# Output projection of a hybrid decoder trunk: pieces of 512, 256 and 256 columns, and the last piece's residual added by products with an identity

## The chip, the core and the metric

The kernel runs on one core of one Trainium2 chip. A core has five engines with a queue of instructions each: TensorE (PE, the matrix products, with a weight-load stage PEld), VectorE (DVE), ScalarE (ACT), GpSimd (POOL) and SyncE (SP, which here only starts transfers). Each works through its own queue in program order and waits on semaphores for the others. Products write into PSUM, which has eight banks of 128 partitions x 512 float32; everything else lies in SBUF or in HBM. The metric is the device time of one execution in microseconds (us): 806.76 us before, the median of 3 runs.

## What is computed

Two decoder layers on 256 tokens of width 1024, in float32. Each normalises the stream, makes one wide projection, runs three token mixers, merges them under gates, and adds an output projection to the stream. Only the end of a layer matters here:

```python
for layer in range(DEPTH):                      # DEPTH = 2
    h = rms_norm(x, norm_w[layer])
    proj = jnp.einsum('bsd,de->bse', h, w_in[layer])
    ...
    branch = jnp.einsum('bsiw,iwd->bsid', ys, w_proj[layer])
    g = jax.nn.sigmoid(gates.reshape(b, s, N_BRANCH, d) + gate_bias[layer])
    merged = jnp.sum(g * branch, axis=2)
    x = x + jnp.einsum('bsd,de->bse', merged, w_out[layer])
return rms_norm(x, final_norm_w)
```

## The kernel before

**Products.** A float32 factor is carried as the sum of two parts in a 32-bit format that PE reads at its full rate (`fp32r`): a high part, copied by ACT, and a low part, the difference, made by DVE (`split`, L287). A product of two factors is three products: high x high, low x high, high x low, for each of the eight k (128 of the 1024 contracted rows). The 256 tokens are two tiles of 128, t = 0 and t = 1; a tile's transposed activations are the stationary side, the weights move.

**Weights** come in blocks of 128 x 1024 numbers (512 KB): `load_part` (L351) starts a transfer on SP's queue into one of six `raw` buffers, and `feed` (L383) splits a block into one of six `hi` and six `lo` buffers. A block of a 256-wide piece holds four k, one of a 512-wide piece two. `feed` runs when a block is released, and no further than `state["limit"]`.

**Order.** PE's order is written out by the code itself: `ops` is a list of steps in program order, and small jobs (`launch`, `pump`, `drain`, L115 to L180) are slipped in between by a clock that adds up the products' estimated lengths. A job's due time is its launch plus a delay, `D_H = (4.8, 6.4)` for the transposes of the next layer's input. DVE's, ACT's and POOL's orders come from the scheduler, in which `tc.high_priority()` and `pin` (L284, keep in program order) intervene.

**The end of a layer.** The last projection piece is merged with its gate, transposed and split (`u_proj`, `merge`, `mT`): the activations `y.mh`, `y.ml` of k = 4 to 7 of t = 1 are the last to be there. In `u_proj` (L1126) the limit is set to two blocks of the output weights before this last merge, then to a third. The output projection follows in three pieces of columns (L1380). The first one, `u_out2`, goes over both tiles in two halves of k: k 0 to 3 of t = 0, of t = 1, then 4 to 7 of each. Its first action is the transposes that are still due of t = 0; between the halves `late` runs the transposes of t = 1 and lifts the limit. The other two pieces are done tile by tile: both of t = 0, then both of t = 1 (L1383).

**Eviction** (`out_end`, L1202). DVE adds the residual `xo` to the bank into `y.xn`; ACT (for the very last piece DVE) sums the squares. After a tile's third piece follow the row's variance, a reciprocal root with a Newton step (`row_rsqrt2`), and, in layer 0, the next layer's input h by two scalings of 512 columns (L1236), whose transposes and splits (`hT`) are a job of the planner; they wait in `drain(5)` and `drain(6)` at the latest, ahead of layer 1's first products. In layer 1 the scaled rows go out by two transfers per tile: 640 columns scaled by DVE and sent by SP, 384 by ACT.

Of the kernel before, what the change touches and what calls it, by code (L numbers as in the profile page):

```python
# [16 lines left out]
P = 128  # L17
# [3 lines left out]
L = 2  # L21
# [29 lines left out]
def hybrid_trunk(  # L51
# [17 lines left out]
    def T(tag, shape, dtype=F32, bufs=None):  # L69
        count[0] += 1  # L70
        return sb.tile(shape, dtype, tag=tag, name=f"{tag}_{count[0]}",
                       bufs=bufs if bufs is not None else BUFS.get(tag, 1))
# [5 lines left out]
    def pmm():  # L78
        return PS("mm", 3)
# [169 lines left out]
    def row_rsqrt2(v, last):  # L249

        r0 = T("sm", [P, 8])
        if last:
            s = T("sm", [P, 8])
            act(s[:, 0:1], v, AF.Sqrt)
            nc.vector.reciprocal(r0[:, 0:1], s[:, 0:1])
        else:
            nc.gpsimd.tensor_tensor(r0[:, 0:1], v, mhalf[:, 0:1], op=ALU.pow)
        a = T("sm", [P, 8])
        stt(a[:, 0:1], r0[:, 0:1], v, r0[:, 0:1], op0=ALU.mult, op1=ALU.mult)
        r = T("rs", [P, 8], bufs=4)  # L260
        stt(r[:, 0:1], a[:, 0:1], -3.0, r0[:, 0:1], op0=ALU.add, op1=ALU.mult)
        return r
# [7 lines left out]
    def in_turn(ap):  # L270
        return ap.rearrange("p (a i) -> p i a", a=2)
# [8 lines left out]
    def halves(ap):  # L280

        return ap.rearrange("p (a i) -> p a i", a=2)

    def pin(f):  # L284
        return lambda *a, **k: tc.keep_in_program_order(f(*a, **k))  # L285
# [217 lines left out]
            if w.last and (k + 1) % w.kper == 0:  # L503
                release(w, k // w.kper + 1)

    def tok(ah, al, w, t, turn=True, mid=None):


        n = w.n
        p = pmm()  # L510
        b = in_turn if turn else lambda ap: ap
        if mid is None and n > 300:
            mid = pump
        dense(p[:, 0:n], lambda k: ah[:, t, k, :], lambda k: al[:, t, k, :], lambda k: b(w.hi(k)),
              lambda k: b(w.lo(k)), w, mid=mid)
        return ordered(p[:, 0:n]) if turn else p[:, 0:n]
# [661 lines left out]
    def u_out(y, c, t, i):  # L1178

        def f(w):  # L1180
            xo = out_start(y, c, t, i, w.n)
            out_end(y, c, t, i, w.n, xo, tok(y.mh, y.ml, w, t))
        return f

    def u_out2(y, c):

# [15 lines left out]
    def out_end(y, c, t, i, n, xo, p):  # L1202
        sl = slice(c, c + n)
        with tc.high_priority():
            tt(halves(y.xn[:, t, sl]), p, halves(xo), op=ALU.add)
            last = y.l + 1 == L
            if last and i == 2:
                junk = T("L2", [P, 512])
                nc.vector.tensor_tensor_reduce(out=junk[:, 0:n], in0=y.xn[:, t, sl], in1=y.xn[:, t, sl],
                                               scale=1.0, scalar=0.0, op0=ALU.mult, op1=ALU.add,  # L1210
                                               accum_out=y.ss[t][:, i:i + 1])
            else:
                sum_sq(y.xn, t, c, y.ss[t][:, i:i + 1], n)
            nwb = fin["w"] if last else layers[y.l + 1].nwb
            if i == 2:
                v = y.var[t][:, 1:2]
                pin(stt)(v, y.ss[t][:, 2:3], 1.0 / D, y.var[t][:, 0:1], op0=ALU.mult, op1=ALU.add)
            if last:
                pin(stt)(y.xn[:, t, sl], y.xn[:, t, sl], -0.5, nwb[:, sl], op0=ALU.mult, op1=ALU.mult)
            else:  # L1220
                nc.scalar.dma_start(xres[t * P:(t + 1) * P, sl], y.xn[:, t, sl])
            if i == 1:
                y.var[t] = row_var(y.ss[t], 2)
            if i == 2:
                r = row_rsqrt2(v, last)
                if last:
                    m = 640
                    ts(y.xn[:, t, 0:m], y.xn[:, t, 0:m], r[:, 0:1], None, op0=ALU.mult)
                    nc.sync.dma_start(out2[t * P:(t + 1) * P, 0:m], y.xn[:, t, 0:m])
                    act(y.xn[:, t, m:D], y.xn[:, t, m:D], AF.Copy, scale=r[:, 0:1])  # L1230
                    nc.scalar.dma_start(out2[t * P:(t + 1) * P, m:D], y.xn[:, t, m:D])
                else:
                    h = layers[y.l + 1].h[t] = T("L4", [P, D])
                    for j in range(2):
                        hs = slice(j * 512, (j + 1) * 512)
                        stt(h[:, hs], y.xn[:, t, hs], r[:, 0:1], nwb[:, hs], op0=ALU.mult, op1=ALU.mult)  # L1236
        if i == 2 and not last:
            launch(5 + t, hT(layers[y.l + 1], t), D_H[t])
        if i == 1:
            pump()  # L1240

    fin = {}

# [19 lines left out]
    def sub(src, n=256):  # L1263
        subs.append((src, n))
        return len(subs) - 1
# [5 lines left out]
    for y in layers:  # L1271
# [105 lines left out]
        op(None, load_final if l + 1 == L else lambda: layer_consts(layers[1], nc.gpsimd))  # L1377
        for f in fox:
            f()
        o = [sub([(0, w_out[l, :, c:c + n])], n) for c, n in ((0, 256), (256, 512), (768, 256))]  # L1380
        pieces_out[l] = o[0]
        op(o[0], u_out2(y, 0))
        for t in range(2):  # L1383
            for i, c in ((1, 256), (2, 768)):
                op(o[i], u_out(y, c, t, i))

    for i, (src, n) in enumerate(subs):
# [204 lines left out]
```

## Time and profile before

| | us |
|---|---|
| median of 3 runs | 806.76 |
| lowest, highest | 806.67, 806.95 |
| span of the profiled execution, first to last instruction | 805.1 |
| busy in it: PE, DVE, ACT, POOL | 796.5, 684.2, 533.8, 167.5 |
| layer 0's output projection on PE, from its first product to layer 1's first | 382.03 to 404.73 |
| layer 1's output projection on PE, first product to the end of the last | 776.84 to 798.84 |
| last instruction of DVE, end | 801.4 |

The profiled execution itself is known by its span; what lies around the span, 1.66 us against the median, is taken to stay as it is. A row of the timeline gives the start in us from the span's start, the busy time, the engine, the line of the kernel (often that of a helper), the operation, what is written and read, the shapes and the number of merged instructions; behind it, in brackets, how long the engine sat idle before and what released it. Instructions overlap at their ends, so from one row's start to the next is often less than the busy time.

### The profile page before, as it was taken

To read this page: it belongs to the slowest core of one execution; us is meant where nothing else is said; L and a number is where in the kernel's file an instruction comes from. 1 tells how busy PE (TensorE), PEld (TensorE's weight loads), DVE (VectorE), ACT (ScalarE), POOL (GpSimd) and SP (SyncE) were. 2 spreads that over 40 slices of the span, in tenths; PEclk is the share of its full clock that TensorE was granted. 3 is DMA by queue.
4 is the path that set the end of the run, shared out by engine and by line. 5 is a ranking of instruction groups with operands and counts; after the bars stand their busy time and mean duration, and the time that the engine had idled before them with its cause. 6 is when DMAs were issued, how large, how long until landed. Compare 5 with 4: busy or idle time off the path is not lost.

```text
span 805.1 us, 14840 instructions
## 1 busy us (share of the span) xinstructions
PE 796.5 (99%) x5160; PEld 711.6 (88%) x5160; DVE 684.2 (85%) x1416; ACT 533.8 (66%) x1146; POOL 167.5 (21%) x236
## 2 busy tenths in 40 slices
PE   9999999999999999999999999999999999999996
PEld 8998988888998988888998899888889989888896
DVE  6878999997998997795785799999889999969865
ACT  7776768875775885543665678687657768755452
POOL 3166213140210100033001741122311220002000
PEclk9999999999999999999999999999999999999999
DMA  9997987797765565686678987679976546576632
GB/s 316 280 259 172 253 219 200 219 290 220 198 184 167 174 187 170 219 253 205 217 251 257 239 210 217 157 217 287 285 211 196 183 143 202 156 248 210 209 106 78
DMA packets 138827, 170.43 MB, mean 212 GB/s; under 512 B 9353, under 2 KB 106465, under 8 KB 138753
## 3 DMA queue, kind: packets, MB, share of 16 engines
q1 hardware_dynamic: 114960, 140.53, 55.5%
q0 software_dynamic: 13328, 13.29, 10.3%
q10 hardware_dynamic: 10464, 15.67, 6.7%
q8 instruction: 41, 0.67, 0.3%
q14 instruction: 34, 0.27, 0.1%
HBM read 154.71 MB, written 2.16 MB: 195 GB/s over the span
## 4 chain that ended last, share of the span: by engine, by line
PE 91%; issue 3%; DMA 2%; POOL 2%; DVE 1%; ACT 1%; POOLq 0%; DVEq 0%
PE mm L109 78%; PE mx L109 9%; PE mx L113 4%; DMA L<-L 1%; DMA hb<-in_sinks_dram 1%; POOL L L488 1%; DMA L<-in_x_dram 0%; DVE L L551 0%; ACT pp L610 0%; POOL L L285 0%; POOL L L562 0%; DVE lo L291 0%; POOL sm L224 0%; POOL L L571 0%; POOL L L572 0%
## 5 line engine op out<-in xcount | busy, mean ns | idle before, releaser
L109 PE MATMUL mm<-L,hi 128*128 128x512 f32 x1056 | 354.7, 387 | 0.5 <-ACT L L487 0.3
L291 DVE TENSOR_TENSOR lo<-raw,hi 128x1024 fp32r<-128x1024 f32 (+1 forms) x276 | 313.3, 1154 | 40.9 <-ACT hi L290 36.1
L109 PE MATMUL mm<-hi,L 128*128 128x512 f32 (+2 forms) x1168 | 303.1, 349 | 0.1
L290 ACT ACTIVATE hi<-raw 128x1024 fp32r<-128x1024 f32 (+1 forms) x276 | 265.6, 982 | 50.6 <-PE mm L109 30.0
L109 PE MATMUL mm<-L,lo 128*128 128x256 f32 x1056 | 266.6, 273 | 0.0
L109 PEld LDWEIGHTS mm<-hi,L 128*128 128x128 f32 x1168 | 205.8, 190 | 23.2 <-issue 1.5
L109 PEld LDWEIGHTS mm<-L,hi 128*128 128x128 f32 x1056 | 195.1, 190 | 27.4 <-issue 3.0
L109 PEld LDWEIGHTS mm<-L,lo 128*128 128x128 f32 x1056 | 202.1, 191 | 5.3
L109 PE MATMUL mm<-lo,L 128*128 128x512 f32 (+2 forms) x584 | 201.5, 347 | 0.0
L109 PEld LDWEIGHTS mm<-lo,L 128*128 128x128 f32 x584 | 110.2, 190 | 10.7
L488 POOL DMA_DIRECT2D L<-L x68 | 60.7, 915 | 192.5 <-ACT L L487 155.2
L1074 POOL TENSOR_SCALAR_AFFINE_SELECT bias<-bias 128x128 f32<-128x128 f32 x64 | 30.8, 513 | 82.7 <-DMA bias<-cumd 82.7
L829 DVE SCALAR_TENSOR_TENSOR L<-L,vec,L 128x255 f32<-128x255 f32 (+2 forms) x96 | 46.2, 481 | 1.9 <-ACT L L826 0.4
L486 ACT ACTIVATE L<-mm 128x256 f32<-128x256 f32 x84 | 31.9, 380 | 20.0 <-PE mm L109 14.0
L652 ACT ACTIVATE pp<-pp,nm 128x128 f32<-128x128 f32 x64 | 28.2, 443 | 22.8 <-DVE nm L646 22.8
L1109 ACT ACTIVATE L<-L 128x512 f32<-128x512 f32 x24 | 15.1, 631 | 34.5 <-DVE L L1106 30.8
L610 ACT ACTIVATE pp<-pp,nm 128x128 f32<-128x128 f32 x32 | 12.6, 394 | 24.9 <-DVE nm L615 24.1
L488 POOL DMA_DIRECT2D qt<-L x16 | 14.2, 925 | 71.4 <-ACT qt L487 64.6
L1142 POOL TENSOR_TENSOR L<-L,L 128x512 f32<-128x512 f32 x8 | 12.0, 1494 | 74.0 <-DVE L L1141 74.0
L487 ACT ACTIVATE L<-mm 128x256 f32<-128x256 f32 x68 | 26.2, 386 | 1.5 <-DMA L<-L 1.5
L1106 DVE TENSOR_TENSOR L<-mm,L 128x512 f32<-128x512 f32 x22 | 15.1, 687 | 11.2 <-PE mm L109 11.2
L551 DVE TENSOR_TENSOR L<-L,cs 128x256 f32<-128x256 f32 x40 | 20.0, 536 | 4.6 <-DMA L<-L 4.6
(213 smaller groups left out, 913.7 us busy)
## 6 DMA issues: line engine op xcount, KB each, us to landing
raw<-in_w_in_dram SPq DMA_DIRECT2D x191, 512.0 KB, 5.1
raw<-in_w_proj_dram SPq DMA_DIRECT2D x48, 512.0 KB, 6.0
L<-L POOLq DMA_DIRECT2D x72, 128.0 KB, 5.4
raw<-in_w_out_dram SPq DMA_DIRECT2D x16, 512.0 KB, 5.9
bias<-cumd ACTq DMA_DIRECT2D x16, 256.0 KB, 3.4
L<-cumd ACTq DMA_DIRECT2D x8, 512.0 KB, 5.4
L<-in_gate_bias_dram ACTq DMA_DIRECT2D x12, 256.0 KB, 5.4
qt<-L POOLq DMA_DIRECT2D x16, 128.0 KB, 6.0
```

What stands on the lines that cost most here:

```text
L109: nc.tensor.matmul(o, a, b, **kw)
L113: nc.tensor.transpose(o, a, i)
L290: keep(act)(hi, src, AF.Copy)
L291: keep(tt)(lo, src, hi.bitcast(F32), op=ALU.subtract)
L486: act(halves(lo), ordered(p[:, S:2 * S]), AF.Copy)
L487: last = act(halves(out), ordered(p[:, 0:S]), AF.Copy)
L488: nc.gpsimd.dma_start(out, lo, accum_op=ALU.add)
L551: tt(m, p, cs[:, i, :], op=ALU.mult)
L652: act(pp[:, i, sl], pp[:, i, sl], AF.Exp, scale=-1.0, bias=nm[:, e:e + 1], accum_out=sums[:, e:e + 1])
L829: stt(a[:, s:S], x_[:, 0:S - s], y.vec[:, 16 * j + u:16 * j + u + 1], a[:, s:S], op0=ALU.mult, op1=ALU.add)
L1074: nc.gpsimd.affine_select(out=bias[:, i, dst], in_=bias[:, i, src], compare_op=ALU.is_ge, fill=NEG, base=0, pattern=[[-1, P]], channel_mul ...
L1106: tt(halves(g), p, halves(y.gb), op=ALU.add)
```

## The change

Three edits.

1. The output pieces (in both layers) are 512, 256 and 256 columns wide, from 256, 512, 256. The first piece, which goes over both tiles in halves of k, is now the wide one. The pieces done tile by tile are both 256 wide.
2. In the last layer, the third piece of t = 1 (`out_last`) no longer adds its residual on DVE. `ahead` loads the residual early, splits it into a high and a low part and copies the identity to `fp32r`; `residual` puts two products with the identity into the middle of the piece, so that the bank holds the sum.
3. Of that bank ACT makes the squares with their sum, and DVE the rows times -0.5 times the final norm's weights; variance and root are taken from the sum directly (`Sqrt` with scale and bias). The scaling and sending of the rows is moved into `send`, unchanged.

```diff
-    def tok(ah, al, w, t, turn=True, mid=None):
+    def tok(ah, al, w, t, turn=True, mid=None, p=None):
...
-        p = pmm()
+        p = p or pmm()
...
         def f(w):
-            xo = out_start(y, c, t, i, w.n)
-            out_end(y, c, t, i, w.n, xo, tok(y.mh, y.ml, w, t))
+            end = (y.l + 1, t) == (L, 1)
+            if end and i == 1:
+                ahead(y)
+            if not (end and i == 2):
+                xo = out_start(y, c, t, i, w.n)
+                out_end(y, c, t, i, w.n, xo, tok(y.mh, y.ml, w, t))
+                return
+            p = pmm()
+
+            def residual():
+                for o in fin["x"]:
+                    mm(p[:, 0:w.n], fin["ident"], in_turn(o), start=False, stop=False)
+            out_last(y, c, t, i, w.n, tok(y.mh, y.ml, w, t, mid=residual, p=p))
         return f
+
+    def ahead(y):
+
+        n = 256
+        xo = T("L1", [P, n])
+        nc.scalar.dma_start(xo, xres[P:S, D - n:D])
+        fin["ident"] = T("L1", [P, P], F32R)
+        nc.gpsimd.tensor_copy(fin["ident"], ident)
+        fin["x"] = [T("L1", [P, n], F32R) for _ in range(2)]
+        split(*fin["x"], xo)
+
+    def out_last(y, c, t, i, n, p):
+
+        sl = slice(c, c + n)
+        with tc.high_priority():
+            junk = T("L2", [P, 512])
+            q = y.ss[t][:, i:i + 1]
+            pin(act)(halves(junk[:, 0:n]), p, AF.Square, accum_out=q)
+            pin(stt)(halves(y.xn[:, t, sl]), p, -0.5, halves(fin["w"][:, sl]), op0=ALU.mult, op1=ALU.mult)
+            s, v, r0 = (T("sm", [P, 8])[:, 0:1] for _ in range(3))
+            pin(act)(s, q, AF.Sqrt, scale=1.0 / D, bias=y.var[t][:, 0:1])
+            pin(stt)(v, q, 1.0 / D, y.var[t][:, 0:1], op0=ALU.mult, op1=ALU.add)
+            pin(nc.vector.reciprocal)(r0, s)
+            send(y, t, newton(v, r0))
...
-        o = [sub([(0, w_out[l, :, c:c + n])], n) for c, n in ((0, 256), (256, 512), (768, 256))]
+        o = [sub([(0, w_out[l, :, c:c + n])], n) for c, n in ((0, 512), (512, 256), (768, 256))]
...
-            for i, c in ((1, 256), (2, 768)):
+            for i, c in ((1, 512), (2, 768)):
```

How the instructions move is shown at three places. **ACT, end of layer 0, around the copies of the last transposes** (`mx`, into the activations `L_913`); `hi` is the high part of a weight block. Before:

```order
L290 ACTIVATE hi_4735<-raw_4589 128x1024
L290 ACTIVATE hi_4747<-raw_4601 128x1024
L1109 ACTIVATE L_947_4698<-L_947_4698 128x512
L285 ACTIVATE hi_4767<-raw_4660 128x1024
L293 ACTIVATE L_913_4525<-mx_4773 128x512
L285 ACTIVATE L_913_4525<-mx_4813 128x512
L285 ACTIVATE hi_4820<-raw_4672 128x1024
```

PE's products behind the transposes of t = 1 (`mx_4813`), now:

```order
L113 MATMUL mx_4813<-ident_71,L_506_2462 128x128 x4
L109 MATMUL mm_4787<-hi_4767,L_913_4525 128x512
L109 MATMUL mm_4787<-hi_4767,L_914_4526 128x512
L109 MATMUL mm_4787<-lo_4768,L_913_4525 128x512
L109 MATMUL mm_4787<-hi_4767,L_913_4525 128x512
L109 MATMUL mm_4787<-hi_4767,L_914_4526 128x512
L109 MATMUL mm_4787<-lo_4768,L_913_4525 128x512
L109 MATMUL mm_4787<-hi_4820,L_913_4525 128x512
```

ACT's rows are the same in the change up to two reads of the residual; but the block `hi_4820`, behind the copy of `mx_4813`, belonged to the second piece before and is the first piece's fourth block now. **PE, from layer 0 to layer 1**: the eight transposes (`x4` twice) of layer 1's input of t = 0. Before, between the second piece (512 wide) and the third (256 wide) of t = 1:

```order
L109 MATMUL mm_4959<-hi_4856,L_914_4526 128x512
L109 MATMUL mm_4959<-lo_4857,L_913_4525 128x512
L113 MATMUL mx_5004<-ident_71,L_995_4954 128x128 x4
L113 MATMUL mx_5011<-ident_71,L_995_4954 128x128 x4
L109 MATMUL mm_5020<-hi_4904,L_913_4525 128x256
L109 MATMUL mm_5020<-hi_4904,L_914_4526 128x256
```

Now, behind both pieces of t = 1 and directly ahead of layer 1's first products (`mm_5071`):

```order
L109 MATMUL mm_5005<-hi_4868,L_914_4526 128x256
L109 MATMUL mm_5005<-lo_4869,L_913_4525 128x256
L113 MATMUL mx_5057<-ident_71,L_995_4954 128x128 x4
L113 MATMUL mx_5064<-ident_71,L_995_4954 128x128 x4
L109 MATMUL mm_5071<-hi_4972,L_1019_5056 128x512 x2
L109 MATMUL mm_5071<-lo_4973,L_1019_5056 128x512
```

The transposes moved past the third piece of t = 1. **DVE at the same place**, from the two scalings of t = 0 (`L_995`) on; `mm_4959` and, before, `mm_5020`, now `mm_5005`, are evictions of t = 1, `lo` are low parts of layer 1's first weights. Before:

```order
L1236 SCALAR_TENSOR_TENSOR L_995_4954<-L_962_4783,rs_4952,L_910_4507 128x512 x2
L291 TENSOR_TENSOR lo_4979<-raw_4771,hi_4978 128x1024
L291 TENSOR_TENSOR lo_4991<-raw_4824,hi_4990 128x1024
L1205 TENSOR_TENSOR L_962_4783<-mm_4959,L_996_4957 128x512
L291 TENSOR_TENSOR lo_5034<-raw_4830,hi_5033 128x1024
L291 TENSOR_TENSOR L_1006_5003<-mx_5004,L_1006_5003 128x4x128
L245 TENSOR_REDUCE sm_5000<-ss_4786 128x1
L291 TENSOR_TENSOR lo_5052<-raw_4860,hi_5051 128x1024
L246 TENSOR_SCALAR sm_5000<-sm_5000 128x1
L291 TENSOR_TENSOR L_1006_5003<-mx_5011,L_1006_5003 128x4x128
L1205 TENSOR_TENSOR L_962_4783<-mm_5020,L_1009_5018 128x256
```

Now:

```order
L1270 SCALAR_TENSOR_TENSOR L_995_4954<-L_962_4783,rs_4952,L_910_4507 128x512 x2
L1243 TENSOR_TENSOR L_962_4783<-mm_4959,L_996_4957 128x256
L294 TENSOR_TENSOR lo_5019<-raw_4830,hi_5018 128x1024
L245 TENSOR_REDUCE sm_5000<-ss_4786 128x1
L294 TENSOR_TENSOR lo_5037<-raw_4836,hi_5036 128x1024
L246 TENSOR_SCALAR sm_5000<-sm_5000 128x1
L1243 TENSOR_TENSOR L_962_4783<-mm_5005,L_1006_5003 128x256
L294 TENSOR_TENSOR lo_5099<-raw_4860,hi_5098 128x1024
L288 SCALAR_TENSOR_TENSOR sm_5000<-ss_4786,sm_5000 128x1
L294 TENSOR_TENSOR lo_5105<-raw_4872,hi_5104 128x1024
L262 SCALAR_TENSOR_TENSOR sm_5049<-sm_5047,sm_5000 128x1
L294 TENSOR_TENSOR L_1019_5056<-mx_5057,L_1019_5056 128x4x128
```

The first split of the transposes (`mx_5004`, now `mx_5057`) stands behind the eviction, four low blocks and the Newton step of t = 1, where before three low blocks and one eviction stood ahead of it. That step reads POOL's power (`sm_5047`).

More of the change, by code (lines that the diff above doesn't have):

```diff
@@ L257, in row_rsqrt2, with newton @@
             nc.gpsimd.tensor_tensor(r0[:, 0:1], v, mhalf[:, 0:1], op=ALU.pow)
+        return newton(v, r0)
+    def newton(v, r0):
         a = T("sm", [P, 8])
@@ L1226, in out_end @@
                 if last:
[L1227 to L1231, printed above, removed]
+                    send(y, t, r)
                 else:
@@ L1240, in out_end, with send @@
             pump()
+    def send(y, t, r):
+        m = 640
+        ts(y.xn[:, t, 0:m], y.xn[:, t, 0:m], r[:, 0:1], None, op0=ALU.mult)
+        nc.sync.dma_start(out2[t * P:(t + 1) * P, 0:m], y.xn[:, t, 0:m])
+        act(y.xn[:, t, m:D], y.xn[:, t, m:D], AF.Copy, scale=r[:, 0:1])
+        nc.scalar.dma_start(out2[t * P:(t + 1) * P, m:D], y.xn[:, t, m:D])
     fin = {}
```

## The prediction

> **What bounds the kernel now.** I read the first part of the page and the chain of waits, then the table by stretches, then the timeline around the two places that the change touches: the end of layer 0 with the start of layer 1, and the end of layer 1.
>
> ```profile
> span 805.1 us, 14840 instructions
> PE 796.5 (99%) x5160; PEld 711.6 (88%) x5160; DVE 684.2 (85%) x1416; ACT 533.8 (66%) x1146; POOL 167.5 (21%) x236
> PE 91%; issue 3%; DMA 2%; POOL 2%; DVE 1%; ACT 1%; POOLq 0%; DVEq 0%
> ```
>
> TensorE (PE) is busy for 99% of the span and owns 91% of the chain. The table by stretches (stretch, its length, then busy time of PE, PEld, DVE, ACT and POOL, granted clock, DMA share, GB/s) says the same of nearly all of layer 1:
>
> ```profile
> 420.00:600.00 180.00, 179.93 (x1199) 161.19 (x1199) 154.04 (x328) 126.12 (x297) 52.48 (x66) 1.00 0.85 232
> 600.00:776.00 176.00, 176.00 (x1096) 155.31 (x1097) 152.47 (x320) 112.10 (x225) 20.34 (x31) 1.00 0.63 194
> ```
>
> In 356 us PE is idle for 0.07. No slack lies there in which a delay of PE could vanish, so a hold at the end of layer 0 reaches the end whole. The question is therefore only: how many products does PE issue, and where does it stand and wait? Rates first:
>
> ```profile
> 790.81 0.60 PE L109 MATMUL mm<-hi,L 128*128 128x512 f32 x2
> 795.99 0.38 PE L109 MATMUL mm<-hi,L 128*128 128x256 f32 x2
> 798.56 0.28 PE L109 MATMUL mm<-lo,L 128*128 128x256 f32 x1
> ```
>
> 24 products of 512 columns are issued between the first two rows: 5.18 / 24 = 0.216 us each. 23 of 256 between the second and third: 2.57 / 23 = 0.112. Two halves cost what one whole does, so the new widths alone leave PE's work as it is.
>
> **The first piece, in both layers.** It is now 512 wide and made of four weight blocks of two k each, instead of two blocks of four k. The planner allows three blocks before the last merge; the fourth (k = 6, 7) is split behind the copy of the second token tile's last transposes. What each step takes, from layer 0 before:
>
> ```profile
> 382.03 0.47 PE L109 MATMUL mm<-hi,L 128*128 128x256 f32 x2
> 384.79 0.60 PE L113 MATMUL mx<-ident,L 128*128 128x128 f32 x4
> 385.43 0.60 ACT L285 ACTIVATE L<-mx 128x512 fp32r<-128x512 f32 x1 [2.52 <-PE mx L113]
> 385.92 2.00 ACT L285 ACTIVATE hi<-raw 128x1024 fp32r<-128x1024 f32 x2
> 399.92 1.06 ACT L290 ACTIVATE hi<-raw 128x1024 fp32r<-128x1024 f32 x1 [0.23 <-PE mm L109]
> 387.11 1.22 DVE L285 TENSOR_TENSOR lo<-raw,hi 128x1024 fp32r<-128x1024 f32 x1
> 386.57 0.61 PE L109 MATMUL mm<-hi,L 128*128 128x256 f32 x2
> 387.02 0.28 PE L109 MATMUL mm<-lo,L 128*128 128x256 f32 x1
> ```
>
> From the start of the four transposes ScalarE (ACT) begins the copy 0.64 later (384.79 to 385.43), the next high block 0.49 after that, and one high block lasts 1.06; VectorE's (DVE) low block lasts 1.22; an engine that was waiting starts 0.04 after its releaser ends (384.79 + 0.60 to 385.43). On before's clock: PE starts the piece at 382.03 and issues 24 products of 512 until 382.03 + 24 x 0.216 = 387.21; the transposes take some 0.36 of issue (387.57); six products of block three bring it to 388.87, where it needs block four's high part. That is ready at 387.21 + 0.64 + 0.49 + 1.06 = 389.40, seen at 389.44: a hold of 0.57. It issues two products (389.87) and needs the low part, which DVE makes from 389.44 to 390.66: PE goes on at 390.70, a hold of 0.83. Together 1.40 us. What it replaces: the pair at 386.57 took 0.45 to the next row instead of 0.22, a hold of 0.23 that goes, since the second tile's split now has 2.6 us of the first tile's products in front of it. Layer 1 has the same order (its table load lies ahead of the transposes), so the same 1.40 and -0.23 apply. Bounds: 0 if the fourth block were not late at all, 2.0 if ACT's and DVE's parts followed without overlap (0.57 + 0.83 + 0.60 for the copy).
>
> **From layer 0 to layer 1.** Before, the first tile's 24 last products (its third piece) were followed by 24 of 512 and 24 of 256 for the second tile, with the eight transposes of the next layer's first tile between the two. Now 48 of 256 follow, and the transposes stand behind all of them. On DVE their low parts stand behind the second tile's chain.
>
> ```profile
> 388.68 2.35 DVE L285 TENSOR_TENSOR lo<-raw,hi 128x1024 fp32r<-128x1024 f32 x2
> 390.94 2.35 DVE L291 TENSOR_TENSOR lo<-raw,hi 128x1024 fp32r<-128x1024 f32 x2
> 396.20 0.42 DVE L1205 TENSOR_TENSOR L<-mm,L 128x256 f32<-128x256 f32 x1 [0.80 <-PE mm L109]
> 397.51 0.58 POOL L257 TENSOR_TENSOR sm<-sm,mhalf 128x1 f32<-128x1 f32 x1 [22.13 <-DVE sm L285]
> 398.57 1.41 DVE L1236 SCALAR_TENSOR_TENSOR L<-L,rs,L 128x512 f32<-128x512 f32 x2
> 399.90 2.35 DVE L291 TENSOR_TENSOR lo<-raw,hi 128x1024 fp32r<-128x1024 f32 x2
> 401.18 1.04 PE L113 MATMUL mx<-ident,L 128*128 128x128 f32 x8
> 401.97 0.47 PE L109 MATMUL mm<-hi,L 128*128 128x256 f32 x2
> 402.27 0.28 PE L109 MATMUL mm<-lo,L 128*128 128x256 f32 x1
> 407.89 1.22 DVE L291 TENSOR_TENSOR lo<-raw,hi 128x1024 fp32r<-128x1024 f32 x1
> 408.06 1.47 POOL L257 TENSOR_TENSOR sm<-sm,mhalf 128x1 f32<-128x1 f32 x1 [9.97 <-DVE sm L285]
> 409.56 0.22 DVE L259 SCALAR_TENSOR_TENSOR sm<-sm,sm 128x1 f32<-128x1 f32 x1 [0.45 <-POOL sm L257]
> 409.82 0.16 DVE L261 SCALAR_TENSOR_TENSOR rs<-sm,sm 128x1 f32<-128x1 f32 x1
> ```
>
> PE first. From 390.70: 4 + 12 products of 512 (3.46) and 96 of 256 (10.72) end their issue at 404.88; the eight transposes take 0.79 (401.18 to 401.97), to 405.67; the first product of layer 1 needs only the high half, so without a hold the second would issue at 405.89.
>
> DVE next. The first tile's last product is issued at about 390.70 + 3.46 + 5.36 - 0.11 = 399.41, and its eviction starts 0.31 later (798.56 to 798.87, below), 399.72. The two row scalings begin 2.37 after that eviction (396.20 to 398.57; POOL's power of 0.58 is in it) and take 1.33 (to 399.90): DVE is free at 403.42. Then, in program order, two evictions of 256 (0.35 each), four low blocks (1.13 each: 388.68 to 390.94 for two) and three small steps (0.08 each) take 0.70 + 4.52 + 0.24 = 5.46; the last block itself ends 0.09 later, 408.97. The next instruction waits for POOL's second power. Before, that power ran beside a low block and the Newton step began 0.45 after the block's end (407.89 + 1.22 = 409.11 to 409.56); 408.97 + 0.45 = 409.42. One step to the next is 0.26, and the split of the transposes, a pass over 128x512, takes 0.70 (half of the 1.41 above): 410.38, seen by PE at 410.42. **Hold: 410.42 - 405.89 = 4.5 us.** Bounds: 4.1 if the Newton step doesn't wait for POOL (less 0.45), 5.4 if the first power also takes 1.47 (0.89 more). I take the middle rows because the first power finds DVE idle as at 397.51, and the second runs beside a low block as at 408.06.
>
> Before, this place cost nothing: the low halves were made while PE still had 24 products to issue. The first pair of 256 behind transposes took 0.30 to the next row (401.97 to 402.27) instead of 0.22; in layer 0 three such places now begin with another shape, in layer 1 two: -0.24 and -0.16 at most. The second tile's halves are not late: PE has 5.2 + 1.3 us of products behind the hold before it transposes them, and DVE needs 1.33 for its scalings and 1.4 for its splits.
>
> **The end of layer 1.** Two products of 256 with the identity join the last bank: 2 x 0.112 = +0.22. Their inputs are prepared in an idle stretch of ACT:
>
> ```profile
> 709.74 0.63 ACT L1109 ACTIVATE L<-L 128x512 f32<-128x512 f32 x1 [3.56 <-DVE L L1106]
> ```
>
> The split of the residual (about 0.4 on ACT, 0.35 on DVE, a cast on POOL) hides there at no cost; uncovered it would be 0.75. The residual reads ahead of the tanh cost ACT's queue some 0.35 each and lie in idle time too; SP issues the same eight transfers of 512 KB in the same places. The last chain:
>
> ```profile
> 782.63 0.41 ACT L241 ACTIVATE L<-L 128x256 f32<-128x256 f32 x1
> 782.94 0.19 ACT L241 ACTIVATION_READ_ACCUMULATOR L<-L 128x1 f32 x1
> 798.87 0.42 DVE L1205 TENSOR_TENSOR L<-mm,L 128x256 f32<-128x256 f32 x1 [0.26 <-PE mm L109]
> 799.80 0.16 DVE L285 SCALAR_TENSOR_TENSOR sm<-ss,sm 128x1 f32<-128x1 f32 x1
> 799.88 0.42 DVE L285 SCALAR_TENSOR_TENSOR L<-L,L 128x256 f32<-128x256 f32 x1
> 800.23 0.16 DVE L255 RECIPROCAL sm<-sm 128x1 f32<-128x1 f32 x1
> 800.87 0.55 DVE L1228 TENSOR_SCALAR L<-L,rs 128x640 f32<-128x640 f32 x1
> ```
>
> Call T the eviction's start, 798.87; the last scaling starts at T + 2.00. Now ACT squares the bank from T, 0.50 with its accumulator (782.63 to 783.13). In the built program DVE's weighting of the same bank waits for ACT's squares, so it doesn't run beside them: T + 0.53, the next step 0.35 later (799.88 to 800.23), reciprocal 0.08 on, T + 0.96, then the same 0.64 to the scaling: T + 1.60. Gain 0.40. Bounds: 0 if reading the bank is slower by that much, 0.59 if the two ran together (the root then ends the wait: 0.50, the 0.27 between the small step's end, 799.96, and the reciprocal, and 0.64 make T + 1.41). The Trainium skill ("PSUM — Partial Sum Buffer", on bank collisions) has two engines kept off one bank at the same time, reads included; by it the overlap isn't to be had and the gain is the 0.40, without it 0.59. No row here shows two such reads at once.
>
> **Sum.** Layer 0: 1.40 + 4.53 - 0.23 - 0.24 = +5.46. Layer 1: 1.40 + 0.22 - 0.23 - 0.16 = +1.23. End: -0.40. Together +6.3 us. The profiled execution's span of 805.1 would become 811.4; the median, 806.76, lies 1.66 above that span, and with the same 1.66 the time is **813.1 us**.
>
> **Rivals.**
> (a) *The clock drops in the hold.* The stretches behind the last product (PE ended at 798.84):
>
> ```profile
> 802.00:803.00 1.00, 0.00 (x0) 0.00 (x0) 0.00 (x0) 0.00 (x0) 0.00 (x0) 0.84 0.69 267
> 803.00:804.00 1.00, 0.00 (x0) 0.00 (x0) 0.00 (x0) 0.00 (x0) 0.00 (x0) 0.50 0.70 257
> ```
>
> 0.84 is 0.68 us at 1 and 0.32 at a half, so the clock halved at 802.68, 3.8 us after work ended. The new hold is longer in sum, 4.5, but one product, released by ACT's copy, stands inside it, so neither idle part reaches 3.8. If it halved all the same, and for as long, 3.8 us at half speed lose 1.9: 815.0. The Trainium skill ("TensorE: Matmul & The Clock Gate", Part 1) has the clock halved after an idle window of about 3.4 us and given back after one of work; the trace's 0.50 and 3.8 agree, and from its figure I estimate 1.7 lost.
> (b) *Only one hold is real.* Without the fourth block's, 2.80 less, 810.3; without that of the transposed halves, 4.53 less, 808.6. For: each rests on one engine's program order. Against: order is fixed when the program is built.
> (c) *Not slower, because something else paces layer 1.* If the weights' DMA, 0.85 busy in 420 to 600, set the pace, PE's records being modelled, layer 0's whole +5.46 would be waited for anyway later; what stays is 1.23 - 0.40: 807.6. It decides from the point where a weight block lands later than PE frees its buffer. Against it: PE's 179.93 of 180.
> (d) *The change doesn't do what its order says:* both holds are covered. Then -0.47, -0.17 and -0.40 remain: 805.7.
>
> **How the numbers follow.** A measurement here tells about 0.2%, 1.6 us, from no change. Forecast 0.70, with its own range from 812.4 (4.1 for the long hold, 0.59 at the end) to 814.7 (5.4, no gain at the end, none from shapes); (a) 0.11; (b) 0.09; (c) 0.05; (d) 0.03; 0.02 is left for a gain that I don't see. The range 810.2 to 815.0 holds the forecast, (a) and the nearer half of (b). Slower: 0.70 + 0.11 + 0.09 = 0.90; same: (c) and (d), 0.08; faster 0.02.
>
> **What would show it.** PE waiting about 0.6 and 0.8 us for block four's high and low part in the middle of the first piece, in both layers; PE waiting some 4.5 us in two parts at the first two products of layer 1, ended by ACT's copy and then by DVE's low half, with DVE at work without a gap over the 5 us before; the last scaling some 1.6 us after PE's last product. A hold at the layer boundary of less than 3 us, or idle PE later in layer 1 that shrinks by what was lost, would prove it wrong.

## The result, and the profile after

The changed kernel takes 815.41 us (median of 4 runs, 815.25 to 815.63) where the kernel before takes 806.86 beside it (806.67 to 807.29): ratio 1.0103, 95% interval 1.0091 to 1.0116. It is slower, as forecast, but by 8.6 us instead of 6.3, just above the upper end of the range. The profiled execution's span is 813.9 us, 8.8 more than before's 805.1.

| | before | after |
|---|---|---|
| median, us | 806.86 | 815.41 |
| span of the profiled execution, us | 805.1 | 813.9 |
| mean granted clock of that execution | 0.998 | 0.996 |
| start of the four transposes of layer 0's first piece | 381.67 | 382.11 |
| start of layer 1's first piece for the second tile | 413.46 | 421.15 |

First the page of after: the span, the engines, and the two groups of PE that stand and wait (busy time, mean ns of one, then the idle time just before them and what ended it).

```profile
span 813.9 us, 14851 instructions
PE 799.7 (98%) x5162; PEld 712.8 (88%) x5162; DVE 683.6 (84%) x1414; ACT 534.5 (66%) x1149; POOL 167.5 (21%) x237
L109 PE MATMUL mm<-hi,L 128*128 128x512 f32 (+2 forms) x1168 | 304.3, 350 | 4.6 <-DVE L L294 2.1
L109 PE MATMUL mm<-lo,L 128*128 128x512 f32 (+2 forms) x584 | 202.4, 348 | 1.1 <-DVE lo L288 1.1
```

PE has two products more (the two with the identity), and 3.2 us more of busy time. Two products of 256 don't take 3.2 us: the same work ran slower somewhere. Beside that stand 5.7 us of waits in two groups, put down to DVE and to rows of L288 and L294.

The timeline of PE in the first piece, layer 0 and then layer 1 (start, length, what, and in brackets the idle time ahead and who ended it):

```profile
389.24 0.38 PE L109 MATMUL mm<-lo,L 128*128 128x512 f32 x1
389.95 0.70 PE L109 MATMUL mm<-hi,L 128*128 128x512 f32 x2 [0.33 <-ACT hi L288]
391.21 0.48 PE L109 MATMUL mm<-lo,L 128*128 128x512 f32 x1 [0.56 <-DVE lo L288]
391.54 0.59 PE L109 MATMUL mm<-hi,L 128*128 128x512 f32 x2
...
792.10 0.70 PE L109 MATMUL mm<-hi,L 128*128 128x512 f32 x2 [0.33 <-ACT hi L288]
793.36 0.48 PE L109 MATMUL mm<-lo,L 128*128 128x512 f32 x1 [0.56 <-DVE lo L288]
```

These are the fourth block's two waits. From start to start the three steps of layer 0 take 0.71, 1.26 and 0.33 instead of 0.22, 0.43 and 0.22: 1.43 us lost; layer 1 loses 1.42.

The layer boundary, PE and DVE:

```profile
405.49 1.04 PE L113 MATMUL mx<-ident,L 128*128 128x128 f32 x8
408.26 0.48 PE L109 MATMUL mm<-hi,L 128*128 128x512 f32 x1 [1.74 <-ACT L L293]
410.85 0.58 PE L109 MATMUL mm<-hi,L 128*128 128x512 f32 x1 [2.10 <-DVE L L294]
411.65 1.06 PE L109 MATMUL mm<-hi,L 128*128 128x512 f32 x2
412.50 0.63 PE L109 MATMUL mm<-lo,L 128*128 128x512 f32 x1
...
408.30 1.22 DVE L294 TENSOR_TENSOR lo<-raw,hi 128x1024 fp32r<-128x1024 f32 x1
409.97 0.22 DVE L262 SCALAR_TENSOR_TENSOR sm<-sm,sm 128x1 f32<-128x1 f32 x1 [0.45 <-POOL sm L257]
410.11 1.28 DVE L294 TENSOR_TENSOR L<-mx,L 128x512 fp32r<-128x512 f32 x2
```

The transposes' issue ends at 405.49 + 0.79 = 406.28. The first product waits for ACT's copy (1.98 us), the second for DVE's low half (2.37 more): 4.35 us, in two parts, with DVE on low blocks, but for 0.45 us of waiting for POOL, up to the split at 410.11. Before, the first half of that split ran while PE still had the third piece of t = 1 to issue:

```profile
403.90 0.69 DVE L291 TENSOR_TENSOR L<-mx,L 128x512 fp32r<-128x512 f32 x1
```

What comes behind the hold is new: the pair that starts at 411.65 takes 0.85 us to the next row instead of 0.43. The table by stretches shows why (busy time of PE, PEld, DVE, ACT, POOL, then the granted clock):

```profile
410.00:411.00 1.00, 0.15 (x1) 0.15 (x2) 1.00 (x3) 0.00 (x0) 0.00 (x0) 1.00 1.00 361
411.00:412.00 1.00, 1.00 (x3) 0.82 (x4) 0.96 (x3) 0.00 (x0) 0.00 (x0) 0.55 0.81 251
...
414.00:415.00 1.00, 1.00 (x4) 0.83 (x4) 0.00 (x0) 0.00 (x0) 0.00 (x0) 0.74 0.78 276
810.00:811.00 1.00, 0.00 (x0) 0.00 (x0) 0.17 (x1) 0.23 (x1) 0.00 (x0) 0.73 0.00 0
```

0.55 is 0.10 us at 1 and 0.90 at a half, so PE's clock halved at 411.10, 0.25 us *after* PE was at work again, and came back at 414.52 (0.74 is 0.52 at a half). The 23 products from 410.85 to the next piece at 417.60 take 6.75 us; at 0.216 they would take 4.97. 1.78 us are lost. The last row is the end of the program, where the clock halves once more, at 810.46. From 414.52 to there it is 395.94 us, 116 times 3.413.

Behind the boundary nothing is made up:

```profile
420.00:600.00 180.00, 179.85 (x1197) 161.28 (x1197) 153.34 (x325) 126.69 (x296) 51.01 (x64) 1.00 0.82 222
600.00:784.00 184.00, 184.00 (x1144) 162.48 (x1143) 158.87 (x329) 117.05 (x234) 21.97 (x34) 1.00 0.66 200
```

The end of layer 1, from the bank's last product at 807.75:

```profile
808.06 0.38 ACT L288 ACTIVATE L<-mm 128x256 f32<-128x256 f32 x1 [1.93 <-PE mm L109]
808.57 0.42 DVE L288 SCALAR_TENSOR_TENSOR L<-mm,L 128x256 f32<-128x256 f32 x1 [1.73 <-ACT L L288]
809.62 0.55 DVE L1278 TENSOR_SCALAR L<-L,rs 128x640 f32<-128x640 f32 x1
```

The last scaling starts 1.56 us after the bank is first read, against 2.00 before: 0.44 gained.

### The profile page after: what moved, and what is told of

It is laid out like the page before. It is cut to its first block, busy times and chain, and to the rows that moved or that the text cites. A ratio compares the mean times of both kernels' runs of the same rounds, so it can differ in the third digit from the quotient of the medians.

```text
span 813.9 us, 14851 instructions
## 1 busy us (share of the span) xinstructions
PE 799.7 (98%) x5162; PEld 712.8 (88%) x5162; DVE 683.6 (84%) x1414; ACT 534.5 (66%) x1149; POOL 167.5 (21%) x237
## 4 chain that ended last, share of the span: by engine, by line
PE 96%; issue 1%; DVE 1%; ACT 1%; DMA 0%; POOL 0%; ACTq 0%; POOLq 0%
PE mm L109 83%; PE mx L109 9%; PE mx L113 4%; DMA L<-in_x_dram 0%; DVE lo L288 0%; ACT hi L288 0%; POOL sm L257 0%; ACT pp L613 0%; DVE L L1492 0%; ACT L L1496 0%; ACT L L1280 0%; DVE L L294 0%; ACT L L241 0%; DVE sm L262 0%; DVE L L1243 0%
## 5 line engine op out<-in xcount | busy, mean ns | idle before, releaser
L294 DVE TENSOR_TENSOR lo<-raw,hi 128x1024 fp32r<-128x1024 f32 (+2 forms) x272 | 308.7, 1152 | 40.8 <-ACT hi L293 36.0
L293 ACT ACTIVATE hi<-raw 128x1024 fp32r<-128x1024 f32 (+2 forms) x272 | 261.8, 982 | 51.0 <-PE mm L109 36.0
L838 ACT ACTIVATE L<-L 128x256 f32<-128x256 f32 x32 | 13.4, 418 | 16.8 <-DVE L L832 16.7
```

The lines of the kernel that those rows point to most:

```text
L293: keep(act)(hi, src, AF.Copy)
L294: keep(tt)(lo, src, hi.bitcast(F32), op=ALU.subtract)
```

## The experiments

Each kernel ran against the kernel before on the same chip. Two theories were open after the traces. The first: the widths alone make two holds, and the idle time of the second is what halves the clock. The second: the clock halves for another reason (a sudden load, the DMA traffic of that moment), or the end has its share in the loss. All times are medians.

| run | us | before, run beside it | ratio, 95% interval | executions, us |
|---|---|---|---|---|
| e1 widths alone | 816.30 | 807.02 | 1.0117 (1.0103 to 1.0130) | 815.68 to 816.80 |
| e2 end alone | 806.65 | 807.02 | 0.9997 (0.9988 to 1.0006) | 806.22 to 807.43 |
| e3 fourth block early | 812.59 | 807.02 | 1.0073 (1.0060 to 1.0085) | 811.80 to 813.52 |
| e4 hold filled | 813.37 | 807.02 | 1.0081 (1.0067 to 1.0095) | 813.00 to 813.87 |
| e5 split ahead of blocks | 810.35 | 807.05 | 1.0042 (1.0029 to 1.0054) | 810.27 to 810.70 |
| e6 both mended | 807.79 | 807.05 | 1.0011 (1.0002 to 1.0020) | 807.42 to 808.32 |
| e7 first half filled | 815.32 | 807.05 | 1.0102 (1.0088 to 1.0115) | 815.05 to 815.34 |
| e8 transposes in the middle | 813.74 | 807.05 | 1.0083 (1.0070 to 1.0096) | 812.16 to 815.05 |
| e9 second half filled | 813.85 | 806.80 | 1.0088 (1.0074 to 1.0102) | 813.53 to 814.35 |
| e10 e6 with the next block ahead | 806.40 | 806.80 | 0.9994 (0.9985 to 1.0002) | 805.61 to 806.89 |
| e11 changed kernel again | 815.24 | 806.80 | 1.0108 (1.0093 to 1.0123) | 814.95 to 816.63 |

**The change in its parts.** e1 is the kernel before with the one line of widths and the column starts that belong to it:

```
-        o = [sub(...) for c, n in ((0, 256), (256, 512), (768, 256))]
+        o = [sub(...) for c, n in ((0, 512), (512, 256), (768, 256))]
-            for i, c in ((1, 256), (2, 768)):
+            for i, c in ((1, 512), (2, 768)):
```

> The kernel before with the new column widths alone; the end is the old one. If the holds come from the widths, this costs what the whole change costs and a little more, since the gain at the end (0.44 read from the two traces, less 0.22 for the two identity products) is missing: 815.6 us, with both holds of the first piece (1.4 each), the 4.4 at the start of layer 1 and about 1.8 lost to a halved clock. Rival: the new end brings part of the loss, then this lies nearer to before's 806.9.

e2 is the changed kernel with these two lines turned back.

> The new end alone, with the old widths 256, 512, 256. If the holds come from the widths, none of them is here, and what stays is -0.44 at the end and +0.22 for the identity products: 806.6 us, last scaling about 1.56 us after PE's last product. Rival: the preparation of the residual or the waits of the new end cost something elsewhere in layer 1, then 807.5 or more.

The whole loss is in the widths: 816.30 for them alone, 806.65 for the end alone. In e2 the end's own gain is seen in the trace; these are PE's last product and DVE's last scaling:

```profile
798.38 0.28 PE L109 MATMUL mm<-lo,L 128*128 128x256 f32 x1
...
800.25 0.55 DVE L1278 TENSOR_SCALAR L<-L,rs 128x640 f32<-128x640 f32 x1
```

From the last product to the last scaling it is 1.87 us, as in the changed kernel (807.75 to 809.62). With the 0.22 for two products more, the net gain of about 0.2 us is less than the runs can tell from nothing. e1 brought a surprise: its median is 0.7 above what was expected, and the trace has its clock at a half for two stretches of 3.42 us, not one (stretches laid on the changes of the clock, at 409.40 and 416.24):

```profile
405.99:409.40 3.41, 0.48 (x1) 0.19 (x1) 2.99 (x6) 1.91 (x5) 1.47 (x1) 1.00 0.89 222
409.40:412.82 3.42, 2.51 (x6) 2.06 (x7) 2.90 (x6) 0.00 (x0) 0.00 (x0) 0.50 0.99 299
412.82:416.24 3.42, 3.42 (x9) 2.69 (x9) 0.00 (x0) 0.00 (x0) 0.00 (x0) 0.50 0.61 209
```

**The fourth block.** In e3 the planner may split it before the last merge:

```
-                limit(j + 1, True)
+                limit(j + 2, True)
```

> The changed kernel with the fourth weight block of the first piece allowed before the last merge, in both layers. If the first piece's hold is nothing but ACT's and DVE's order (the block's high and low part stand behind the copy and split of the second tile's transposes), PE finds them ready and 2 x 1.42 us go: 812.6 us, no idle PE in the first piece. Rival: the wait only moves, since the block's two passes now stand ahead of the second tile's copy and split, or its buffer isn't free so early; then 814 to 815.4. The hold at the start of layer 1 and its halved clock stay.

812.59 where 812.6 was expected (the executions spread over 1.7 us, so that they agree to 0.01 is luck), and PE's rows at that place follow each other at 0.43 and 0.22 without a wait:

```profile
389.25 0.38 PE L109 MATMUL mm<-lo,L 128*128 128x512 f32 x1
389.46 0.59 PE L109 MATMUL mm<-hi,L 128*128 128x512 f32 x2
389.89 0.38 PE L109 MATMUL mm<-lo,L 128*128 128x512 f32 x1
```

So that hold was the order of ACT and DVE and nothing else, 2.8 us for both layers.

**The clock.** e4 keeps PE busy while it waits:

```
+            def fill():
+                state["bank"] = p = pmx()
+                for _ in range(17):
+                    nc.tensor.transpose(p[:, 0:P], ident, ident)
+                state["fill"] = 21
             op(None, lambda: drain(5))
+            op(None, fill)
...
                 mm(pt, a(k), b(k), start=..., stop=...)
+                for _ in range(state.pop("fill", 0)):
+                    nc.tensor.transpose(state["bank"][:, 0:P], ident, ident)
```

> The changed kernel with 38 idle transposes of the identity on PE inside the hold at the start of layer 1: 17 ahead of the first product, 21 between the first and the second, at 0.099 us each 1.7 and 2.1 us of the 4.4. Nobody reads them; all that is computed stays. If PE's idle time is what halves its clock, the clock stays at 1.00, the first piece's products take 0.216 us each instead of 0.43, and 1.7 us are won although the hold is as long as before: 813.7 us. Rival: the clock falls for another reason (a sudden load, the DMA traffic of 0.9 to 1.0 share at that place), then it falls here too and the time stays 815.4. Third: the fill itself makes the hold longer, by up to 0.3.

The hold is as long as in the changed kernel, the clock stays at 1, and 2.0 us are won. PE's timeline around the first two products, then the stretch behind them (granted clock 1.00, DMA share 0.91):

```profile
405.79 2.02 PE L1382 MATMUL mx<-ident 128*128 128x128 f32 x17
407.69 0.48 PE L109 MATMUL mm<-hi,L 128*128 128x512 f32 x1
408.01 2.46 PE L313 MATMUL mx<-ident 128*128 128x128 f32 x21
410.27 0.48 PE L109 MATMUL mm<-hi,L 128*128 128x512 f32 x1
```

```profile
410.00:415.00 5.00, 5.00 (x27) 4.39 (x26) 2.30 (x5) 0.00 (x0) 0.00 (x0) 1.00 0.91 286
```

The first product still starts 1.98 after the transposes' issue (404.92 + 0.79), the second 2.58 after the first, and the DMA engines are as busy there as in the changed kernel (0.93 from 410 to 415): the traffic doesn't halve the clock. The idle transposes take the sudden step of load away as well as the idle time, so this run alone can't tell those two apart. But at the end of the program the clock halves with no load behind it at all, and in e9 (below) the load sets in after a wait and the clock stays up. PE's idleness is what is left. e7 asks how much of it: it fills the first part only (without the line that sets 21).

> The changed kernel with the first 17 of the idle transposes only: PE works until the first product, then stands for 2.35 us in one stretch. Nobody reads them; all that is computed stays. If the clock is set by how much PE works in fixed windows of 3.41 us that run on their own, a window that holds the stretch whole is 31% work and one that holds half of it 65%: the clock falls in some executions and stays in others, 815.2 or 813.4 us, by where the windows happen to lie. Rival: what counts is an unbroken idle stretch as long as the window; then it never falls, and all executions lie at 813.4.

The rival of that expectation fell, and the expectation itself came half true: it had the clock stay up in some executions. PE stands still only once, for 2.36 us of issue (2.10 by the row), and the clock halves in all four executions (815.05 to 815.34, mean granted clock 0.996). PE's row behind the gap:

```profile
410.58 0.48 PE L109 MATMUL mm<-hi,L 128*128 128x512 f32 x1 [2.10 <-DVE L L294]
```

And two stretches laid on the change of the clock at 411.80:

```profile
408.39:411.80 3.41, 1.31 (x7) 1.09 (x7) 2.92 (x6) 0.04 (x1) 1.28 (x1) 1.00 0.92 269
411.80:415.21 3.41, 3.41 (x10) 2.65 (x9) 0.84 (x2) 0.00 (x0) 0.00 (x0) 0.50 0.89 300
```

The clock halves when PE has been back at work for 1.2 us, and stays down for 3.41: what counts is how much PE did in a window, not the length of one idle stretch. e9 fills the second part only (it sets 21 and leaves the loop of 17 out).

> The changed kernel with the 21 idle transposes between the first and the second product only; the 1.98 us ahead of the first product stay empty. Nobody reads the transposes; all that is computed stays. The windows of the runs so far were followed by half speed with 36% of work in them (the half filled hold) and with 37% (a second low window in the run of the widths alone, work counted at half), and by full speed with 44% and 46% (the low windows of the middle and of the fourth block's run, counted so). A window that holds the 1.98 whole is 42% work: if about 40% is the bound, the clock stays up in nearly all executions and the time is 815.4 - 1.8 = 813.6 us. Rival: the bound lies above 42%, then about half of the executions lose 1.4 us more, up to 815.

All four executions lie between 813.53 and 814.35, with a mean clock of 0.998 or 0.999; no execution lost the 1.4. The wait of 1.98 is there (PE's timeline). The clock doesn't fall before the program's end; counted back from its change there, at 809.07, in steps of 3.413, the window with the least work around the wait is this one, 54% busy:

```profile
407.87 0.48 PE L109 MATMUL mm<-hi,L 128*128 128x512 f32 x1 [1.73 <-ACT L L293]
```

```profile
406.30:409.71 3.41, 1.84 (x15) 1.78 (x16) 2.96 (x7) 1.75 (x5) 1.47 (x1) 1.00 0.82 233
```

e11 is the changed kernel once more, unedited.

> The changed kernel once more. If the loss of clock hangs on where free-running windows of 3.41 us lie over the hold, it is one low window in some executions and two in others: 1.3 to 3.1 us over the 813.5 without a loss, so executions between 814.8 and 816.6 whose mean clock is 0.996 or 0.994. Rival: the loss is a fixed 1.8, and all executions lie within 0.4 of 815.4.

Its executions are 814.95, 814.99, 815.49 (mean clock 0.996) and 816.63 (0.994): by these means one window of 3.41 us at half clock (a low window), or two. A fixed loss, which would put all within 0.4, is out.

**The layer boundary.** e8 puts the transposes of the next layer's first tile in the middle of the second tile's last piece:

```
+                early = (y.l, t, i) == (0, 1, 2)
-                out_end(y, c, t, i, w.n, xo, tok(y.mh, y.ml, w, t))
+                out_end(y, c, t, i, w.n, xo, tok(y.mh, y.ml, w, t, mid=(lambda: drain(5)) if early else None))
```

> The changed kernel with the transposes in the middle of the last piece and nothing else: their low parts stand behind three of the four blocks instead of behind all of them and the second tile's first Newton step. The second product's low half comes some 1.9 us earlier, a hold of about 2.5 us instead of 4.4: 813.5 us where the clock falls for one window, 811.7 where it doesn't. Rival: the hold is set by the first product's high half, ACT's copy behind the high block; then the hold moves by less than 0.5.

The first product of layer 1 comes nearly at once, the second 3.02 after it (2.8 lost, against 2.5 expected), since three low blocks and an eviction still stand ahead of the split. The executions spread over 2.9 us: 812.16 with a mean clock of 0.998, 813.50 to 814.35 with 0.996, 815.05 with 0.994. By these means that is none, one, or two low windows behind the same hold. In the profiled one, PE's first two products, and the window in which the clock was down:

```profile
406.77 0.48 PE L109 MATMUL mm<-hi,L 128*128 128x512 f32 x1
409.79 0.79 PE L109 MATMUL mm<-hi,L 128*128 128x512 f32 x1 [2.54 <-DVE L L294]
```

```profile
409.42:412.83 3.41, 3.04 (x7) 2.49 (x8) 2.89 (x7) 0.00 (x0) 1.47 (x1) 0.50 0.97 318
```

e5 does the same and takes three of the four blocks out of the split's way:

```
+            if (y.l, t, i) == (0, 1, 2):
+                state["limit"] = state["split"] + 1
...
-            split(hTh[...], hTl[...], pv)
+            split(hTh[...], hTl[...], pv, keep=keep)
...
             op(None, lambda: drain(5))
+            op(None, lambda: limit(None, True))
             op(cv0, u_cv(y, 0, 0))
+            op(None, lambda: state.update(pin=False))
```

> The changed kernel with the backlog taken out of VectorE's way at the layer boundary: the eight transposes of the next layer's first tile stand in the middle of the second tile's last piece, their low parts are pinned, and only one weight block instead of four is split between the first tile's scalings and them. If the hold at the start of layer 1 is DVE's backlog, the second product's low half is there at about 406.8 on the changed kernel's clock: a hold of about 0.3 instead of 4.4, no halved clock (1.8), but the three blocks that were put back come late: block four's low part and block five's stand behind the second tile's scalings, about 0.5 and 0.7 of new waits. 815.4 - 4.4 - 1.8 + 1.5 = 810.7 us. Rival: the first tile's scalings or the transposes themselves are what is late, not the blocks; then the hold stays above 3 us and the time above 813. The first piece's holds stay.

The timeline of DVE and of PE:

```profile
405.41 1.28 DVE L288 TENSOR_TENSOR L<-mx,L 128x512 fp32r<-128x512 f32 x2
410.20 1.22 DVE L288 TENSOR_TENSOR lo<-raw,hi 128x1024 fp32r<-128x1024 f32 x1
...
406.01 0.62 PE L109 MATMUL mm<-hi,L 128*128 128x512 f32 x2
411.48 0.48 PE L109 MATMUL mm<-lo,L 128*128 128x512 f32 x1 [0.97 <-DVE lo L288]
```

The split starts at 405.41 instead of 410.11, and PE goes from layer 0 into layer 1 without a stop (406.01 follows the last product of layer 0 at once). e8 had moved the split ahead of the fourth block and the second tile's step and still lost 2.8 us; with two more blocks out of its way (and its place pinned) nothing of that is left. That DVE's queue ahead of the split was the hold is thereby shown. A smaller wait takes its place where it was expected: block four's low part, now behind the second tile's scalings, starts at 410.20 and holds PE for 1.13 from row to row. The fifth block was not late. The clock stays up; 810.35 us.

e6 is e3 and e5 together.

> The edits of the fourth block and of the split ahead of the blocks together, with the new widths and the new end. If the two holds are independent, the gains add up: 810.7 - 2.8 = 807.9 us, within 0.2% of the kernel before; PE waits only for the blocks that were put back. Rival: with the first piece 1.4 us earlier, the blocks come that much later for PE, and part of the gain is given back: 809 us.

807.79 where 807.9 was expected: the two gains add up, to within 0.1 us. e10 takes the last wait away by letting one more block follow the split at once:

```
-                out_end(y, c, t, i, w.n, xo, tok(y.mh, y.ml, w, t, mid=(lambda: drain(5)) if early else None))
+                mid = (lambda: (drain(5), limit(state["split"] + 1, True))) if early else None
+                out_end(y, c, t, i, w.n, xo, tok(y.mh, y.ml, w, t, mid=mid))
```

> As the run with both places mended, but the next weight block follows right behind the split of the transposes, so that it stands ahead of the second tile's chain (and the two behind it between the steps of that chain) instead of behind its scalings. If the wait left there (0.97 for block four's low part and 0.17 around it) is only this order, it goes: 807.8 - 1.1 = 806.7 us, no different from the kernel before. Rival: the chain of the second tile now comes late for its transposes in the second piece; then PE waits there and the time stays near 807.8.

DVE's row of that block:

```profile
405.69 1.22 DVE L288 TENSOR_TENSOR lo<-raw,hi 128x1024 fp32r<-128x1024 f32 x1
```

The block's low part now starts at 405.69 (the split at 404.16), and between 380 and 418 us no product of PE waits. 806.40 us against 806.80: with both orders mended the new widths cost nothing that can be measured, and bring nothing either. No run here is measurably faster than the kernel before.

## Why the forecast was right in its direction and too low

Point by point, in the prediction's own terms, against the profiled spans (805.1 and 813.9):

| term | forecast | measured |
|---|---|---|
| fourth block, both layers | +2.80 | +2.85; taken away in e3, 2.8 us go |
| layer boundary | +4.53 | +4.35; gone in e5 |
| pair that waited for the second tile's split (-0.23 in each layer) | -0.46 | -0.46: 0.45 to the next row before, no wait after |
| shapes behind transposes | -0.40 | -0.08 (below) |
| identity products | +0.22 | +0.22: two more products |
| the last chain | -0.40 | -0.44 |
| clock in the hold (a rival, 0.11) | 0 | +1.78 |
| start of the first piece | 0 | +0.44 |
| sum | +6.3 | +8.7, of 8.8 |

The two holds are where they were put, ended by the engines that were named, and within 0.2 us of their size. Of the rivals, (b) fell with the two holds. (c) fell with the stretches from 420 to 784, in which PE is idle for 0.15 us. (d) fell in e1. The last row but one is no effect of the change: in the thirteen traces of this study that piece starts anywhere between 381.19 and 382.34, e11's, which is the same kernel, at 381.96.

**The step that failed** is the dismissal of rival (a): "one product, released by ACT's copy, stands inside it, so neither idle part reaches 3.8". That 3.8 had been read at the program's end as an idle time that must run unbroken before the clock halves. It is not one. In the changed kernel neither part was longer than 2.37 and the clock halved, and in e7 it halved behind a single stop of 2.36. What the runs show in its place: the clock is set anew every 3.413 us, by how much PE did in the window just past; the windows run on their own, whatever the program does. In all thirteen traces the changes of the clock, from its first rise between 6 and 11 us to its fall behind the last product, lie whole multiples of 3.413 us apart, up to 235 of them. At the end of the kernel before, PE's work ended 0.43 us ahead of a window's edge, and the 3.8 was that 0.43 and one empty window. The Trainium skill ("TensorE: Matmul & The Clock Gate", Part 1) has the window free-running and 3413 ns long; the 116 windows between two changes in one trace agree. Its rule for kernels, in the same part under "HAM oscillation — how this bites in real kernels", is to leave no idle gap above about 3.4 us; here 2.36 (2.10 by the row) was enough, so the measurement narrows it.

How little work is too little is bracketed by windows of these traces, with the work counted as the busy time of the rows. At full clock, 0.48 of 3.41 us (14%) ahead of e1's first low window and 1.31 (38%) in e7 were followed by half speed, and so was the window in which e8's products end, 41% busy (the clock halves at 808.77):

```profile
805.36:808.77 3.41, 1.39 (x13) 1.20 (x11) 1.54 (x8) 1.20 (x4) 0.00 (x0) 1.00 0.20 73
```

e9's 1.84 (54%) was followed by full speed. So the bound lies between 41% and 54%. At half clock, 2.51 (73%) in e1's first low window was followed by half speed again, 3.04 (89%) in e8's by full speed. If work at half clock is counted half, these are 37% and 45%, and one bound between 41% and 45% fits all of these windows. The counting by halves is argued from two windows, not shown. e9's other executions fit too: a window that holds all of its 1.73 us of idle is still 49% busy. So does the fourth block's hold, which never cost clock: with its 0.33 and 0.56 of idle a window is 74% busy. e7 fits less well: by an estimate from its 2.10 us of idle and that bound, about half of the possible places of the window would have kept the clock, and all four executions lost it. With four, that can be chance; where exactly the bound lies stays open.

With such windows the changed kernel's hold leaves the clock little chance. By the rows PE is idle in it for 1.74 + 2.10 = 3.84 us, with one product between. Either a window lies wholly inside it, or two neighbours of 6.83 us cover it and have 6.83 - 3.84 = 2.99 us of work between them, 44% on the mean; unless they share it almost evenly, one of them falls under 41%. All eight executions of the changed kernel lost clock (mean clock 0.996, once 0.994). Rival (a) was not a chance of 0.11 but the likeliest case. Its own price, 1.9, was right to 0.1, in part by luck: it took 3.8 us at half speed, where one low window has 3.41 and some executions have two. With that price and 0.08 for the shapes the forecast would have been 815.3.

**One term was mis-sized.** Of the 0.40 for shapes behind transposes 0.08 came. The first pair behind the transposes takes 0.08 more to the next row whatever its width, as the changed kernel's timeline has it:

```profile
382.11 0.60 PE L113 MATMUL mx<-ident,L 128*128 128x128 f32 x4
382.46 0.68 PE L109 MATMUL mm<-hi,L 128*128 128x512 f32 x2
382.98 0.38 PE L109 MATMUL mm<-lo,L 128*128 128x512 f32 x1
383.19 0.59 PE L109 MATMUL mm<-hi,L 128*128 128x512 f32 x2
383.62 0.38 PE L109 MATMUL mm<-lo,L 128*128 128x512 f32 x1
```

0.52 from the second row to the third, 0.43 from the fourth to the fifth. And it is no price at all: eight transposes take 0.79 us when a product follows (401.18 to 401.97 in the kernel before) but 0.87 when more transposes do (404.92 to 405.79 in e4), so the row of the first product starts 0.08 early and the one behind the pair is where it would be anyway. The 0.08 that did go is that of the pair behind layer 0's eight transposes, where PE now waits.

## What to carry to other kernels

When an order is changed on the engine that everything waits for, look at what the engines beside it have queued ahead of the one result that is now due sooner: one hold here was a weight block behind the copy and split of activations, the other four blocks of 1.1 us and a step of the second tile ahead of a split. Changing that order took both away, though the next block behind the split then had to be moved too. A hold on TensorE is not paid by its own length alone: add up PE's busy time in any 3.4 us around it, and where that can fall to some 40% (41% was too little here, 54% was enough), add one window of half speed or two (e11's executions lie 1.6 to 3.3 us above e4, which has the same hold without it). Idle products in the wait bring that part back, but not the hold.

## What the runs showed of the hardware beside this

The same hold behind the same code costs different executions different amounts, by where the windows happen to lie: e8's five executions are 812.16 to 815.05 us with mean clocks of 0.998 to 0.994, while e5's, which has no such hold, lie within 0.43 us. A spread of that kind between executions can be a sign of a hold near the bound. And half speed can keep itself up: in e1 PE was busy for 2.51 of 3.42 us in a low window, 73% of the time, and the clock stayed down for the window behind it.
